# A float32 encoder block: the MLP's low parts all on VectorE, its unscaled stream kept in DRAM, the first gate products and the last stage's operands moved ahead

## The chip, the cores and the metric

The kernel runs on one core of a Trainium2 chip. The metric is the device time of one execution in microseconds (us). The kernel before took 1575.88 us (median of 3 runs, 1573.33 to 1576.59).

## What is computed

One encoder block on 1024 frames with 16 learned meta tokens in front, 1024 features wide, all in float32. A token mixer comes first and the change leaves it alone. What matters here is the gated MLP behind it and the final norm:

```
h = h + token_mixer(rmsnorm(h, g_mix))
u = rmsnorm(h, g_ffn)
a = causal_dwconv(u @ w_up, ffn_conv_w)          # 3 taps along time
h = h + (silu(a) * (u @ w_gate)) @ w_down        # 1024 -> 2816 -> 1024
out = rmsnorm(h, g_final)[:, 16:]                # rmsnorm(x,g) = x / sqrt(mean(x*x) + 1e-6) * g
```

## The kernel before

**Products in three parts.** TensorE (PE) multiplies in the reduced type fp32r. Every float32 operand is therefore split into a high part, a cast that ScalarE (ACT) makes, and a low part, the operand minus its high part. `mm3s` (L552) then issues three matmuls for each 128x128 weight block: high by high, high by low, low by high (L558 to L560). A split of weights is `wsplit` (L238, cast L242, subtraction L243); a split of activations is `rsplit` (L563, cast L565, subtraction L566). `wsplit` takes the engine of the subtraction as an argument. The mixer's output product and the whole down stage hand it VectorE (DVE). In the MLP `fstep` (L247) hands it VectorE for the first three units of weights and GpSimd (POOL) for all later ones.

**Seven products for eight.** Each large product is done by a scheme that needs seven block products instead of eight, from sums of weight blocks and sums of activation blocks. `fstep` makes the weight sums on VectorE (L261 to L263, L266), `xcomb` (L1035) the activation sums. The class `Seven` (L572) runs the products with w_out and w_down; `seven` (L1200) those with w_up and w_gate.

**The MLP.** The 2816 hidden features are 22 blocks of 128, taken as 11 pairs. Pair 0 is done with plain products while the activation sums are still being made (`first_up`, `first_gate`, L1300 to L1310); its results wait in DRAM and are finished by `first_out` (L1293) after pairs 1 to 4, one quarter after each. For pairs 1 to 10 `up_part` (L1312) makes seven products with w_up, each in two chunks of some 256 columns, and `gate_part` (L1323) seven with w_gate, each of 512 columns. The list PROD (L1199) says for each product which bank, weight unit and activation block it uses: the first two use blocks 0 and 1, which are plain, the third and fourth use sums that `xcomb` makes. ScalarE copies three of the intermediate banks to SBUF (tiles S0, S2 and S3, L1226), VectorE adds to them (L1230). The fifth product accumulates onto the bank that S2 was copied from, so it waits for that copy.

From a finished quarter of w_up `conv` (L1240) makes the depthwise convolution: one multiply (L1244) and two multiply-adds (L1246) on VectorE, Silu on ScalarE (L1247), and a multiply by Rb on GpSimd (L1248). `gate` (L1288) multiplies by the gate's quarter on VectorE and stores the result to DRAM.

**Why the multiply by Rb.** Rb holds 1/rms of each column. `scale_tasks` (L1075) scales the stream `resid` in place by Rb before the MLP, so the MLP's output has to be scaled too before it is added back to it (L1248). The final norm is then taken of a scaled stream: L1390 turns Rb into the epsilon that belongs to the scaled columns, `sq` (L1418) adds the squares onto it, and `final_rms` (L1426) calls `rms` with eps=False.

**The down stage.** It loops over five steps ("1", "2", "65", "73", "4") of 11 blocks each (L1391 to L1411 and L1445 to L1451). `prep` (L627) splits one step's operands ahead of its products `mms` (L674), one step early. After "73" `give` (L686) adds eight banks to `resid`. The last step "4" splits its w_down quarter when it comes to it, runs half of the columns inside the loop and the other half in `last_quarter` (L692) in two groups of 256.

**The end.** The final norm comes in three pieces of columns, 512, 256 and 256 (OP, L1416). For each, squares on ScalarE (L1423) are added on VectorE (piece 0) or GpSimd (pieces 1 and 2, L1424). `rms` (L297) sums over the partitions with matmuls (L304), takes the root (L310) and the reciprocal (L311), spreads the result over all partitions with matmuls into PSUM (L316), and copies it to Rb (L319). `final_out` (L1431) multiplies the blocks by gain and Rb: some in one instruction on VectorE (L1442), the others on ScalarE (gain, L1439) and GpSimd (Rb, L1440), and stores them.

**What sets the order.** Every engine, and the queue of SyncE (SP) that issues all DMAs, takes its instructions in order. The order is not that of the source: a scheduler built into the tile framework simulates the program and orders each engine's instructions by when they would be ready in that simulation. `after` (L81) adds an order between two instructions without a wait. Buffers come from rings of fixed length: split weights hi and lo 3 each (L131), raw weights 2, S tiles 5 (L1022), and two rings of four PSUM banks (L1055).

Of the kernel before, what the change touches and what calls it, by code (L numbers as in the profile page):

```python
# [17 lines left out]
P = 128  # L18
# [43 lines left out]
def body(ctx, tc, h_in, vecs, cst, mask_in, rot, w_v0, w_v, w_fm, w_out, w_up, w_gate, w_down, out):  # L62
# [172 lines left out]
    def fsplit(nm, srcs, eng=None):  # L235
        return wsplit(*split_tiles(nm), srcs, eng)

    def wsplit(hi, lo, srcs, eng=None):  # L238
        o = 0
        for x in srcs:  # L240
            n = x.shape[1]
            nc.scalar.copy(hi[:, o:o + n], x)  # L242
            (eng or nc.gpsimd).tensor_tensor(lo[:, o:o + n], x, hi[:, o:o + n].bitcast(F32), ALU.subtract)  # L243
            o += n
        return hi, lo

    def fstep(u, s):  # L247
# [6 lines left out]
        eng = V if u < 3 else None  # L254
        if u < 2:
            return fsplit(nm, [(r0, r1)[s]], eng)
        if s == 0:
            return fsplit(nm, [r0], eng)
        if s == 1:
# [37 lines left out]
    def rms(ss, t0, t1, nm, col, rb, ptags=("tr", "num"), eps=True):  # L297
# [5 lines left out]
        for i, (o, w) in enumerate(subs):  # L303
            nc.tensor.matmul(pc[:w, i:i + 1], ss[:, o:o + w], cs[:, C_M01 + P - 1:C_M01 + P], start=True, stop=True)  # L304
# [5 lines left out]
        nc.scalar.activation(col[:, i0:ns], pc[:, i0:ns], AF.Sqrt, bias=epsc if eps else 0.0, scale=1.0 / D)  # L310
# [8 lines left out]
        nc.scalar.copy(rb[:, x:], pr[:, :n - x])  # L319
# [243 lines left out]
    def rsplit(x, tiles):  # L563
        hi, lo = (t[:, :x.shape[1]] for t in tiles)
        nc.scalar.copy(hi, x)  # L565
        V.tensor_tensor(lo, x, hi.bitcast(F32), ALU.subtract)  # L566
        return hi, lo

# [3 lines left out]
    class Seven:  # L572
# [30 lines left out]
        def pre4(self, t):  # L603
# [3 lines left out]
            for i in range(2):  # L607
                self.four[t + i] = wsplit(*self.wfour(k + i), [x[:, i * HB:(i + 1) * HB]], V)
# [14 lines left out]
        def tsum(self, i, k):  # L623
            a, b, c = {1: ("A1", "B1", "A1"), 3: ("B1", "B1", "B2")}[i]
            V.tensor_tensor(self.act[a, k], self.act[b, k], self.act[c, k], ALU.subtract)

        def prep(self, t):  # L627
# [7 lines left out]
            if st == "4" and self.wfour:  # L635
# [4 lines left out]
            elif st == self.order[-1]:  # L640
                if k % 2 == 0:
                    self.w = d["w"]
                w = wsplit(*self.wlast(k), [self.w[:, k % 2 * HB:(k % 2 + 1) * HB]], V)
                self.ops[t] = [(w, self.rhalf(k, 0), "xy"[st == "2"])]
            elif st in self.QUARTER:
                if k % 2 == 0:
                    self.w = fsplit(nm, [d["w"]], V)
                r = rsplit(act[{"1": "A1", "2": "A2", "4": "A1"}[st], k], self.rt(st, k, 0))
                self.ops[t] = [(half_of(self.w, k % 2), r, "xy"[st == "2"])]
            elif st == "65":  # L650
# [3 lines left out]
                w = fsplit(nm, [d["l"]], V)  # L654
# [3 lines left out]
            else:  # L658
                w = fsplit(nm, [d["l"]], V)
# [5 lines left out]
        def rhalf(self, k, half):  # L665
            x = self.act["A2" if self.order[-1] == "2" else "A1", k][:, half * QT:(half + 1) * QT]
            return rsplit(x, self.rlast(k) if half else self.rt(self.order[-1], k, 0))
# [532 lines left out]
    def seven(kind, i, chunks, done):  # L1200

        S = {}
# [3 lines left out]
        for n, (bank, s, o, x) in enumerate(PROD):  # L1206
# [30 lines left out]
            elif n == 6:  # L1237
                done(1, 0, [banks["x", ci][:, :j1 - j0] for ci, (j0, j1) in enumerate(chunks)])

    def conv(i, m, half, c):  # L1240
        t0 = (TA, TB)[half]
# [6 lines left out]
        nc.gpsimd.tensor_tensor(cv, cv, Rb[:, t0 + 2:t0 + XW], ALU.mult)  # L1248
# [63 lines left out]
    def up_part(i):  # L1312
# [8 lines left out]
        seven("up", i, chunks, done)  # L1321

    def gate_part(i):  # L1323
        def done(m, half, c):
            gate(i, m, half, c[0] if isinstance(c, list) else c[:, :HALF])
        seven("ga", i, [(2, XW)], done)
        if i < 5:
            first_out((i - 1) % 2, (i - 1) // 2)
# [22 lines left out]
    def draw_(st, nm):  # L1351
        return raw_tile(nm) if st == "1" else dps["d"].tile([P, 2 * HB], F32, tag="draw", name="r" + nm, bufs=4)
# [7 lines left out]
    def dwlast(k):  # L1360
        if k < 6:
            if k % 2 == 0:
                dw4[k // 2] = split_tiles(f"d4_{k}")
            return half_of(dw4[k // 2], k % 2)
# [178 lines left out]
```

## Time and profile before

| | |
|---|---|
| median of 3 runs | 1575.88 us |
| time of the profiled execution | 1575.3 us |
| its span, first to last instruction | 1573.2 us |
| mean granted TensorE clock | 0.99 |
| PE / VectorE / ScalarE / GpSimd busy | 97 / 74 / 45 / 18% |
| HBM read and written | 142.25 and 45.13 MB, 119 GB/s |

Times in the trace count from the span's start. The mixer runs to about 740 us, its output product to about 875, the MLP's pair 0 to 920, its pairs 1 to 10 to about 1345, the down stage to 1561, and the end follows. A PE that the profile calls busy is not always at full speed: the granted clock has two levels, 2.4 GHz (shown as 1.00) and 1.2 GHz (0.50), and a stretch's mean lies between.

### The profile page before, as it was taken

How to read it: one execution, taken by the hardware profiler on the slowest of the kernel's cores; microseconds unless marked ns; L12 is line 12 of the kernel's file. 1: busy time of each engine (PE TensorE's matmuls, PEld its weight loads, DVE VectorE, ACT ScalarE, POOL GpSimd, SP SyncE). 2: the span in 40 equal slices, each digit the busy share in tenths (PEclk: the TensorE clock that was granted, in tenths of full speed). 3: DMA queues.
4: the chain of work that ended last, by engine and by line, in shares of the span. 5: the costliest groups of instructions: out<-in, count | busy, mean ns of one | idle time of the engine just before them, and what ended most of it. 6: DMA issues, size and time to landing. Idle time of an engine off the chain costs nothing.

```text
span 1573.2 us, 25559 instructions
## 1 busy us (share of the span) xinstructions
PE 1528.0 (97%) x9749; PEld 1398.2 (89%) x9749; DVE 1157.6 (74%) x2318; ACT 711.4 (45%) x1457; POOL 283.1 (18%) x195
## 2 busy tenths in 40 slices
PE   7999999999999999999999999999999999999996
PEld 6999999999999999997888988888999998888886
DVE  8767768597868686779976788877766666776575
ACT  6574655545242425355455453333333334333363
POOL 0000000000000000000000006666666665000006
PEclk9999999999999999999999999999999999999999
DMA  6125435262625353245430122222222224832312
GB/s 211 41 69 166 149 116 180 86 217 93 217 79 191 105 160 129 88 154 194 177 121 27 34 88 101 85 91 74 81 81 81 81 81 162 320 115 88 105 61 107
DMA packets 88315, 189.04 MB, mean 120 GB/s; under 512 B 8504, under 2 KB 29696, under 8 KB 88192
## 3 DMA queue, kind: packets, MB, share of 16 engines
q1 hardware_dynamic: 88192, 187.41, 35.3%
q8 instruction: 76, 1.25, 0.3%
q14 instruction: 47, 0.39, 0.1%
HBM read 142.25 MB, written 45.13 MB: 119 GB/s over the span
## 4 chain that ended last, share of the span: by engine, by line
PE 79%; DVE 8%; DMA 7%; ACT 3%; issue 2%; POOL 1%; SPq 0%; DVEq 0%; ACTq 0%; POOLq 0%
PE pv L380 3%; PE pv L381 3%; PE pv L382 3%; PE pga_x L558 2%; PE pup_x L559 2%; PE po L391 2%; PE po L392 2%; PE po L390 2%; PE pup_x L558 2%; PE pup_x L560 2%; PE pga_x L559 2%; PE pga_x L560 2%; PE pdx L559 2%; PE pdx L560 2%; PE pdx L558 2%
## 5 line engine op out<-in xcount | busy, mean ns | idle before, releaser
L1248 POOL TENSOR_TENSOR cv<-cv,Rb 128x512 f32<-128x512 f32 x44 | 67.6, 1541 | 980.3 <-ACT cv L1247 967.9
L380 PE MATMUL pv<-hi_v,uh 128*128 128x256 f32 (+1 forms) x512 | 146.5, 286 | 7.6 <-DVE uh L278 7.6
L382 PE MATMUL pv<-hi_v,ul 128*128 128x256 f32 (+1 forms) x512 | 144.9, 284 | 1.9 <-DVE ul L281 1.8
L381 PE MATMUL pv<-lo_v,uh 128*128 128x256 f32 (+1 forms) x512 | 145.4, 284 | 0.0
L390 PE MATMUL po<-uh,hi_o 128*128 128x386 f32 (+2 forms) x384 | 125.1, 326 | 0.0
L391 PE MATMUL po<-ul,hi_o 128*128 128x386 f32 (+2 forms) x384 | 123.2, 321 | 0.0
L392 PE MATMUL po<-uh,lo_o 128*128 128x386 f32 (+2 forms) x384 | 122.9, 320 | 0.0
L380 PEld LDWEIGHTS pv<-hi_v,uh 128*128 128x128 f32 x512 | 97.1, 190 | 10.3 <-ACT hi_v L149 7.2
L382 PEld LDWEIGHTS pv<-hi_v,ul 128*128 128x128 f32 x512 | 96.6, 189 | 2.4 <-DVE ul L281 2.3
L381 PEld LDWEIGHTS pv<-lo_v,uh 128*128 128x128 f32 x512 | 96.9, 189 | 1.0 <-DVE lo_v L150 0.9
L243 POOL TENSOR_TENSOR lo_ga<-fraw_ga,hi_ga 128x512 fp32r<-128x512 f32 (+1 forms) x50 | 87.8, 1765 | 43.9 <-ACT hi_ga L242 43.9
L243 POOL TENSOR_TENSOR lo_up<-raw_up,hi_up 128x512 fp32r<-128x512 f32 (+1 forms) x45 | 74.0, 1654 | 47.4 <-ACT hi_up L242 47.4
L242 ACT CAST hi_up<-raw_up 128x512 fp32r<-128x512 f32 (+1 forms) x52 | 36.5, 720 | 97.0 <-PE pga_z L559 45.7
L390 PEld LDWEIGHTS po<-uh,hi_o 128*128 128x128 f32 x384 | 72.5, 189 | 0.1
L391 PEld LDWEIGHTS po<-ul,hi_o 128*128 128x128 f32 x384 | 72.4, 188 | 0.2
L392 PEld LDWEIGHTS po<-uh,lo_o 128*128 128x128 f32 x384 | 72.2, 188 | 0.0
L559 PE MATMUL pup_x<-ul_g,hi_up 128*128 128x256 f32 (+1 forms) x240 | 68.2, 286 | 1.0 <-DVE ul_g L1011 1.0
L558 PE MATMUL pup_x<-uh_g,hi_up 128*128 128x256 f32 (+1 forms) x240 | 68.0, 285 | 0.6 <-ACT uh_g L1010 0.6
L560 PE MATMUL pup_x<-uh_g,lo_up 128*128 128x256 f32 (+1 forms) x240 | 66.7, 284 | 0.0
L390 PE MATMUL pq<-uh,hi_q 128*128 128x400 f32 (+2 forms) x192 | 63.9, 333 | 2.3 <-DVE vl L356 1.2
L242 ACT CAST hi_ga<-fraw_ga 128x512 fp32r<-128x512 f32 (+1 forms) x52 | 36.4, 718 | 62.4 <-PE pup_z L559 48.2
L390 PE MATMUL pk<-uh,hi_k 128*128 128x400 f32 (+2 forms) x192 | 62.4, 325 | 0.3 <-DVE rq L411 0.3
(733 smaller groups left out, 5198.9 us busy)
## 6 DMA issues: line engine op xcount, KB each, us to landing
wsd<-w_down_d SPq DMA_DIRECT2D x22, 512.0 KB, 4.2
wsd<-wsd SPq DMA_DIRECT2D x44, 256.0 KB, 2.3
raw_up<-w_up_d SPq DMA_DIRECT2D x22, 512.0 KB, 3.6
fraw_ga<-w_gate_d SPq DMA_DIRECT2D x22, 512.0 KB, 3.6
acts<-cv SPq DMA_DIRECT2D x44, 256.0 KB, 2.0
rd<-wsd SPq DMA_DIRECT2D x22, 512.0 KB, 3.2
wsw<-w_out_d SPq DMA_DIRECT2D x16, 512.0 KB, 4.2
raw_o<-w_fm_d SPq DMA_DIRECT2D x16, 512.0 KB, 3.5
```

The source lines that it names most:

```text
L242: nc.scalar.copy(hi[:, o:o + n], x)
L243: (eng or nc.gpsimd).tensor_tensor(lo[:, o:o + n], x, hi[:, o:o + n].bitcast(F32), ALU.subtract)
L380: nc.tensor.matmul(pv[:L, :nv], a, hi[:, o:o + nv], start=kb == 0, stop=False)
L381: nc.tensor.matmul(pv[:L, :nv], a, lo[:, o:o + nv], start=False, stop=False)
L382: nc.tensor.matmul(pv[:L, :nv], b, hi[:, o:o + nv], start=False, stop=kb == KB - 1)
L390: nc.tensor.matmul(pt[:, :n], a, uh[kb][:, t0:t1], start=kb == 0, stop=False)
L391: nc.tensor.matmul(pt[:, :n], a, ul[kb][:, t0:t1], start=False, stop=False)
L392: nc.tensor.matmul(pt[:, :n], b, uh[kb][:, t0:t1], start=False, stop=kb == KB - 1)
L558: m.append(nc.tensor.matmul(pt, ah, xh_, start=first and k == 0, stop=False, skip_group_check=True))
L559: nc.tensor.matmul(pt, ah, xl_, start=False, stop=False, skip_group_check=True)
L560: m.append(nc.tensor.matmul(pt, al, xh_, start=False, stop=last and k == n - 1, skip_group_check=True))
L1248: nc.gpsimd.tensor_tensor(cv, cv, Rb[:, t0 + 2:t0 + XW], ALU.mult)
```

## The change

- `wsplit` has no engine argument any more: VectorE makes every low part.
- `conv` makes its first multiply on ScalarE, and the multiply by Rb is gone. In its place `norm_tasks` (L1064) stores each block of the unscaled stream to DRAM, 24 DMAs in all, before it is scaled, and pairs 3 to 10 each end with one DMA of 512 KB that brings one block of it back to `resid`.
- In pair 1 the gate's first two products come behind the up product's first two; the unit of weights that they need, (3, 0), is split before (2, 1).
- In the down stage the last step's weights of blocks 6 to 10 are loaded and split during step "73", into memory that held activations; the first three blocks of the last step are prepared before `give`, the others three ahead instead of one. The second halves of the last step's activations are split in the loop, ordered behind the splits of the first halves, and the sums `tsum` are ordered behind the latest `rsplit`.
- In the end all adds of squares go to VectorE; in piece 2 the last block's squares are not added but summed by matmuls of their own. Pieces 0 and 1 are multiplied by the factor where it lies in PSUM, without the copy, all on VectorE. In piece 2 VectorE does the same for six blocks; for blocks 1 and 4 ScalarE applies the gain ahead of time and GpSimd the factor. Each piece is stored in four DMAs.

```diff
-    def wsplit(hi, lo, srcs, eng=None):
+    def wsplit(hi, lo, srcs):
...
-            (eng or nc.gpsimd).tensor_tensor(lo[:, o:o + n], x, hi[:, o:o + n].bitcast(F32), ALU.subtract)
+            nc.vector.tensor_tensor(lo[:, o:o + n], x, hi[:, o:o + n].bitcast(F32), ALU.subtract)
...
     fu = [(u, s) for u in range(len(fseq)) for s in range(2 if u < 2 else 4)]
+    fu.insert(fu.index((2, 1)), fu.pop(fu.index((3, 0))))
...
         for i, (o, w) in enumerate(subs):
-            nc.tensor.matmul(pc[:w, i:i + 1], ss[:, o:o + w], cs[:, C_M01 + P - 1:C_M01 + P], start=True, stop=True)
+            for a in (ss, *more):
+                nc.tensor.matmul(pc[:w, i:i + 1], a[:, o:o + w], cs[:, C_M01 + P - 1:C_M01 + P], start=a is ss, stop=a is (ss, *more)[-1])
...
-        nc.scalar.copy(rb[:, x:], pr[:, :n - x])
+        if rb is not None:
+            nc.scalar.copy(rb[:, x:], pr[:, :n - x])
+        return pr[:, :n - x]
...
             nc.scalar.activation(dst, resid[:, mb, t0:t1], AF.Square)
+            u0 = max(t0, META)
+            nc.sync.dma_start(stream[:, mb, u0 - META:t1 - META], resid[:, mb, u0:t1])
...
+            if n == 1:
+                yield
...
-        nc.vector.tensor_scalar(cv, c[:, 2:XW], vec[:, w + 2:w + 3], None, ALU.mult)
+        nc.scalar.activation(cv, c[:, 2:XW], AF.Copy, scale=vec[:, w + 2:w + 3])
...
         nc.scalar.activation(cv, cv, AF.Silu)
-        nc.gpsimd.tensor_tensor(cv, cv, Rb[:, t0 + 2:t0 + XW], ALU.mult)
...
     for i in range(1, NPAIR):
-        up_part(i)
+        u, g = up_part(i), gate_part(i)
+        next(u)
+        if i == 1:
+            next(g)
+        run(u)
...
-        gate_part(i)
+        run(g)
+        if 2 < i:
+            kb = i - 3
+            nc.sync.dma_start(resid[:, kb, META:], stream[:, kb])
...
-    nc.scalar.activation(Rb[:, META:], Rb[:, META:], AF.Square, scale=math.sqrt(EPS * D / P))
...
-            down.tsum(1, t - 2)
+            after(down.tsum(1, t - 2), last["rsplit"][1])
...
+        if st == "73":
+            for u, v in ((2, 6), (3, 8), (5, 10)):
+                if k == u:
+                    down.load(T4 + v)
+                if k == u + 2:
+                    down.pre4(T4 + v)
         down.mms(t)
         if k == KD - 1:
+            if st == "73":
+                for u in range(T4, T4 + 3):
+                    down.prep(u)
             down.give(st)
...
-        (G if p else V).tensor_tensor(ss, ss, dst, ALU.add)
+        if p == 2 and mb == KB - 1:
+            lastsq.append(dst)
+        else:
+            V.tensor_tensor(ss, ss, dst, ALU.add)
...
+        for mb in pool:
+            nc.gpsimd.tensor_tensor(resid[:, mb, a0:t1], resid[:, mb, a0:t1], R[1], ALU.mult)
...
-                if mb in pool:
-                    nc.scalar.activation(x, x, AF.Copy, scale=g)
-                    nc.gpsimd.tensor_tensor(x, x, R, ALU.mult)
-                else:
-                    nc.vector.scalar_tensor_tensor(x, x, g, R, ALU.mult, ALU.mult)
+                if mb not in pool:
+                    V.scalar_tensor_tensor(x, x, vec[:, V_FIN + mb:V_FIN + mb + 1], R[0], ALU.mult, ALU.mult)
...
-    down.prep(T4)
     for k in range(KD):
         down.load(T4 + k + 4)
-        down.prep(T4 + k + 1)
+        down.prep(T4 + k + 3)
+        down.late[k] = down.rhalf(k, 1)
         down.mms(T4 + k)
...
-            final_rms(0)
-            final_out(0, (1, 3, 5, 7), (0, 4, 8))
-        final_rms(p)
-        final_out(p, (1, 3, 5, 7) if p == 1 else (2, 5, 7), (0, 4, 8) if p == 1 else (0, 3, 6, 8))
+            final_out(0, final_rms(0), (), (0, 2, 4, 6, 8))
+        else:
+            for mb in (1, 4):
+                x = resid[:, mb, OP[2][0]:OP[2][1]]
+                nc.scalar.activation(x, x, AF.Copy, scale=vec[:, V_FIN + mb:V_FIN + mb + 1])
+        final_out(p, final_rms(p), (1, 4) if p == 2 else (), (0, 2, 4, 6, 8))
```

## Rows read from the trace of the kernel before

**Rows 1.** Two long stretches of the MLP: length, engines' busy time, granted clock.

```profile
942.00:1110.00 168.00, 159.38 (x970) 141.94 (x969) 133.83 (x147) 58.12 (x109) 107.46 (x67) 0.97 0.27 90
1110.00:1330.00 220.00, 219.95 (x1393) 197.91 (x1391) 152.93 (x182) 80.03 (x151) 146.63 (x90) 1.00 0.25 84
```

**Rows 2.** What PE waited for, 820 to 1345 us: total us, times, longest.

```profile
PE pga_x L558 <- ACT s2ga L1226: 9.4, 5, 2.7
```

**Rows 3.** Timeline of ScalarE, 947 to 963 us; idle time in brackets.

```profile
959.38 1.29 ACT L1247 ACTIVATE cv<-cv 128x512 f32<-128x512 f32 x2 [6.02 <-DVE cv L1246]
960.58 0.57 ACT L1226 COPY s2ga<-pga_x 128x512 f32<-128x512 f32 x1
```

**Rows 4.** VectorE's groups, 942 to 1330 us: count, busy us, mean ns.

```profile
L261 DVE TENSOR_TENSOR s<-raw_up 128x512 f32<-128x512 f32 x9 | 16.0, 1781 | 0.0
...
L1246 DVE SCALAR_TENSOR_TENSOR cv<-s3up,vec,cv 128x512 f32<-128x512 f32 x20 | 14.9, 745 | 0.0
...
L1244 DVE TENSOR_SCALAR cv<-s0up,vec 128x512 f32<-128x512 f32 x9 | 4.4, 487 | 0.3
```

**Rows 5.** VectorE's low parts while GpSimd rests, 1345 to 1520 us.

```profile
L243 DVE TENSOR_TENSOR lo_d<-rd,hi_d 128x1024 fp32r<-128x1024 f32 x27 | 33.0, 1221 | 29.2 <-ACT hi_d L242 29.2
...
L243 DVE TENSOR_TENSOR lo_d<-rd,hi_d 128x512 fp32r<-128x512 f32 x3 | 2.0, 690 | 3.7 <-ACT hi_d L242 3.7
```

**Rows 6.** GpSimd's groups, 942 to 1330 us: first and last of six of L243.

```profile
L243 POOL TENSOR_TENSOR lo_ga<-fraw_ga,hi_ga 128x512 fp32r<-128x512 f32 x40 | 63.8, 1608 | 25.8 <-ACT hi_ga L242 25.8
...
L243 POOL TENSOR_TENSOR lo_ga<-s,hi_ga 128x512 fp32r<-128x512 f32 x10 | 14.8, 1475 | 0.0
```

**Rows 7.** Timeline of VectorE, 947 to 962 us: start, us, what.

```profile
951.01 1.79 DVE L261 TENSOR_TENSOR s<-raw_up 128x512 f32<-128x512 f32 x1
...
959.27 0.74 DVE L1246 SCALAR_TENSOR_TENSOR cv<-c0b,vec,cv 128x512 f32<-128x512 f32 x1
```

**Rows 8.** Short stretches around PE's pauses, columns as in rows 1.

```profile
930.00:942.00 12.00, 9.49 (x44) 8.06 (x43) 7.37 (x16) 6.18 (x13) 2.80 (x2) 0.72 0.15 44
958.00:966.00 8.00, 5.27 (x18) 3.97 (x17) 6.79 (x8) 3.17 (x5) 5.30 (x3) 0.79 0.39 131
1002.00:1010.00 8.00, 6.05 (x24) 4.64 (x23) 6.78 (x8) 3.17 (x5) 5.30 (x3) 0.79 0.37 132
1044.00:1048.00 4.00, 2.01 (x10) 1.32 (x8) 3.96 (x7) 1.82 (x4) 1.14 (x1) 1.00 0.04 5
1086.00:1096.00 10.00, 8.05 (x33) 6.28 (x32) 8.79 (x10) 3.17 (x5) 5.28 (x3) 0.83 0.28 101
...
1524.00:1530.00 6.00, 4.13 (x32) 3.66 (x31) 6.00 (x13) 3.69 (x8) 0.00 (x0) 1.00 0.00 1
1552.00:1554.00 2.00, 0.63 (x6) 0.42 (x5) 2.00 (x4) 0.17 (x1) 2.00 (x2) 1.00 0.96 369
```

**Rows 9.** ScalarE's groups, 1530 us to the end.

```profile
L1439 ACT ACTIVATE resid<-resid,vec 128x512 f32<-128x512 f32 x3 | 2.2, 717 | 0.0
...
L319 ACT COPY Rb<-prc 128x256 f32<-128x256 f32 x2 | 0.7, 364 | 1.1 <-PE prc L316 1.1
```

**Rows 10.** A stretch of the down stage, columns as in rows 1.

```profile
1345.00:1520.00 175.00, 175.00 (x756) 141.82 (x755) 120.25 (x169) 74.33 (x113) 0.00 (x0) 1.00 0.39 138
```

**Rows 11.** DMA issues: count, KB each, median us to landing.

```profile
acts<-cv SPq DMA_DIRECT2D x44, 256.0 KB, 2.0
```

**Rows 12.** Timeline of PE, 1560.6 us to the end.

```profile
1563.03 0.61 PE L304 MATMUL pcc<-cs,Rb 128*128 128x1 f32 x4 [1.90 <-POOL Rb L1424]
```

**Rows 13.** VectorE's groups, 1530 us to the end.

```profile
L1442 DVE SCALAR_TENSOR_TENSOR resid<-resid,vec,Rb 128x256 f32<-128x256 f32 x9 | 7.1, 846 | 2.6 <-ACT Rb L319 2.6
...
L705 DVE TENSOR_TENSOR resid<-pdx,resid 128x256 f32<-128x256 f32 x8 | 3.1, 418 | 4.4 <-PE pdx L560 4.4
```

**Rows 14.** Timeline of SP's DMA queue, 850 to 880 us.

```profile
860.51 9.55 SPq L231 DMA_DIRECT2D fraw_ga<-w_gate_d  x3
```

**Rows 15.** Timeline of VectorE, 855 to 862 us.

```profile
856.27 4.93 DVE L1082 TENSOR_TENSOR resid<-resid,Rb 128x514 f32<-128x514 f32 x8 [4.89 <-ACT Rb L319]
```

More of the change, by code (lines that the diff above doesn't have):

```diff
@@ L233, in fetch, with fsplit @@
         fraws[u] = r
[L235 to L238 removed]
+    def fsplit(nm, srcs):
+        return wsplit(*split_tiles(nm), srcs)
+    def wsplit(hi, lo, srcs):
         o = 0
@@ L295, in sumsq, with rms @@
         return spare_tile("ss", "ss" + nm)
-    def rms(ss, t0, t1, nm, col, rb, ptags=("tr", "num"), eps=True):
+    def rms(ss, t0, t1, nm, col, rb, ptags=("tr", "num"), more=()):
         n = t1 - t0
@@ L561, in mm3s, with rsplit, behind @@
         return m[0], m[-1]
-    def rsplit(x, tiles):
+    def rsplit(x, tiles, late=False):
         hi, lo = (t[:, :x.shape[1]] for t in tiles)
-        nc.scalar.copy(hi, x)
-        V.tensor_tensor(lo, x, hi.bitcast(F32), ALU.subtract)
+        m = nc.scalar.copy(hi, x), V.tensor_tensor(lo, x, hi.bitcast(F32), ALU.subtract)
+        if late:
+            behind(m)
+        else:
+            last["rsplit"] = m
         return hi, lo
+    def behind(m):
+        for x, y in zip(m, last["rsplit"]):
+            after(x, y)
     def half_of(u, o):
@@ L606, in pre4 @@
             x = self.draws[t]["w"]
-            for i in range(2):
-                self.four[t + i] = wsplit(*self.wfour(k + i), [x[:, i * HB:(i + 1) * HB]], V)
+            for i in range(x.shape[1] // HB):
+                self.four[t + i] = wsplit(*self.wfour(k + i), [x[:, i * HB:(i + 1) * HB]])
             self.read(t, True)
@@ L634, in prep @@
             act = self.act
-            if st == "4" and self.wfour:
+            if st == "4" and self.order[-1] != "4":
                 if t not in self.four:
@@ L641, in prep @@
                 if k % 2 == 0:
-                    self.w = d["w"]
-                w = wsplit(*self.wlast(k), [self.w[:, k % 2 * HB:(k % 2 + 1) * HB]], V)
+                    self.w = d.get("w")
+                w = self.four.get(t) or wsplit(*self.wlast(k), [self.w[:, k % 2 * HB:(k % 2 + 1) * HB]])
                 self.ops[t] = [(w, self.rhalf(k, 0), "xy"[st == "2"])]
@@ L666, in rhalf @@
             x = self.act["A2" if self.order[-1] == "2" else "A1", k][:, half * QT:(half + 1) * QT]
-            return rsplit(x, self.rlast(k) if half else self.rt(self.order[-1], k, 0))
+            return rsplit(x, self.rlast(k) if half else self.rt(self.order[-1], k, 0), half and self.nm == "d")
         def bank(self, b, j, new=False):
@@ L1060, in fps @@
         return pp(nm, ring[-1])
+    stream = dram.tile([P, KB, SEQ], F32, name="stream")
     def norm_tasks(t0, t1, mbs=range(KB), first=True):
@@ L1087, in run @@
         for f in fs:
-            f()
+            if f:
+                f()
     for p in range(3):
@@ L1320, in done @@
             conv(i, m, half, c)
-        seven("up", i, chunks, done)
+        return seven("up", i, chunks, done)
     def gate_part(i):
@@ L1325, in done @@
             gate(i, m, half, c[0] if isinstance(c, list) else c[:, :HALF])
-        seven("ga", i, [(2, XW)], done)
-        if i < 5:
-            first_out((i - 1) % 2, (i - 1) // 2)
+        return seven("ga", i, [(2, XW)], done)
     dps = {}
@@ L1360, in dwlast, with dfour @@
     def dwlast(k):
[L1361 to L1364, printed above, removed]
-        return tuple(dps["e"].tile([P, HB], F32R, tag=f"w4{x}{k}", name=f"w4{x}{k}") for x in "hl")
+        if k % 2 == 0:
+            dw4[k // 2] = split_tiles(f"d4_{k}")
+        return half_of(dw4[k // 2], k % 2)
+    def dfour(k):
+        r = []
+        for i in (2 * k - 12, 2 * k - 11):
+            tag = ("ul1", "uh2", "ul2")[i // 4]
+            if tag not in dw4:
+                dw4[tag] = upool.tile([P, 2 * T], F32R, tag=tag, name=f"{tag}_w4")
+            r.append(dw4[tag][:, i % 4 * HB:(i % 4 + 1) * HB])
+        return tuple(r)
     down = Seven("d", KD, w_down, ("1", "2", "65", "73", "4"), META, draw_, drt,
@@ L1403, in body @@
         if 2 <= t < KD + 2:
-            down.tsum(1, t - 2)
+            after(down.tsum(1, t - 2), last["rsplit"][1])
         if KD + 4 <= t < 2 * KD + 4:
-            down.tsum(3, t - KD - 4)
+            after(down.tsum(3, t - KD - 4), last["rsplit"][1])
         if st != "1" or k + 4 < KD:
             down.load(t + 4)
+        if st == "73":
[4 more added lines that the diff above has]
+                    down.pre4(T4 + v)
         down.mms(t)
         if k == KD - 1:
+            if st == "73":
+                for u in range(T4, T4 + 3):
+                    down.prep(u)
             down.give(st)
```

44 lines of the change are left out of this document (24 added, 20 removed).

## The prediction, made before the changed kernel had run

> **What bounds the kernel now.** I read the busy shares, then the busy time by stretch, then the pauses of PE, the waits behind them and what the late engines did. PE is busy nearly throughout, so VectorE, ScalarE and GpSimd matter only where they make PE pause. In pairs 5 to 10 PE has no pause: 219.95 of 220 us; in the stretch of pairs 1 to 4 it lacks 8.6 of 168 us and its clock is 0.97 [rows 1]. The reader is to see that a pause costs twice: PE stands still, and the clock is then granted at its lower level (1.2 of 2.4 GHz) for some us. A stretch of length L at mean clock c does L(1-c) less work.
>
> Who is late? Most of the waiting in the MLP is one product waiting for ScalarE's copy S2 [rows 2]. At 958 us ScalarE sat idle 6.02 us until VectorE had finished two convolutions, ran two Silus, and only then copied S2 [rows 3], though the bank had been complete for some time. VectorE was late because it ran beside GpSimd: a plain two-input instruction on 128x512 takes 1781 ns there [rows 4], with GpSimd at rest 690 [rows 5]. A multiply-add of the convolution takes 745 where it is undisturbed [rows 4]. Pairs 1 to 4 carry one quarter of pair 0 more each than pairs 5 to 10, and VectorE is busy 80% there (133.83 of 168) against 70% (152.93 of 220) [rows 1].
>
> **The change, part by part.** All sums are against the profiled execution: 1575.3 us, that is 1573.2 of span and 2.1 around it; the median of the runs is 0.6 higher.
>
> *Low parts and multiplies, pairs 1 to 10.* VectorE gains 95 subtractions of 512 columns and 19 of 1024 (six groups of L243 [rows 6]): 95 x 0.690 + 19 x 1.221 [rows 5] = 88.7 us. It loses 43 multiplies (L1244, 487 ns where undisturbed [rows 4]), and GpSimd's 254.1 us [rows 1] disappear, with the slowing of VectorE. The 286 VectorE instructions that stay (329 less 43 [rows 1]) cost, undisturbed, 86 x 0.745 (conv) + 143 x 0.690 (512 columns) + 57 x 0.42 (256) = 186.7 us. So VectorE goes from 286.8 to about 275 of 388 us, 71%; in pairs 1 to 4 to about 73%, near the 70% at which pairs 5 to 10 run without a pause now. The slowing is worth 286.8 - 186.7 - 43 x 0.487 = 79 us; if half of it stayed, VectorE would be busy 81%: that is what the slower rival is made of.
>
> The chain to S2 at 958 us, redone: from 951 to the end of the last conv instruction VectorE took 9.0 us [rows 7]. Undisturbed and without the two multiplies that is 2 x 0.69 + 4 x 0.745 = 4.4 us. The low parts add 88.7 / 388 of the time, 2.1 us in 9. So it ends 2.5 us earlier in the same order, while PE's pause was 2.73 [rows 8]. But the order is made anew by a simulation that plainly did not count on the slowing, and now nothing is left that slows VectorE. I take these pauses as gone but for one of 2 us.
>
> Their price [rows 8]: idle 2.73 + 1.95 + 1.99 + 1.95 = 8.6; clock 8 x 0.21 + 8 x 0.21 + 0 + 10 x 0.17 = 5.1. Together 13.7, of which I count 11.7. The bounds are a gain of 13.7 and a loss, in the slower rival.
>
> *ScalarE's multiplies.* 43 at 0.717 [rows 9] are 30.8 us more on an engine busy 138.2 of 388 us [rows 1]; 44% after. Hidden by its idle time; without that cover it delays S2, the same rival. Here a rule speaks against the change. An undisturbed multiply costs VectorE 487 ns [rows 4] and ScalarE 717 [rows 9], 0.23 us more each, 9.9 us in all, off PE's path. The Trainium skill ("ScalarE: Activation LUTs", Rules for kernel authors) tells authors to do a plain multiply on VectorE and not on ScalarE; by it this part would be a loss of those 9.9 us of engine time. The trace bears out the prices, not that they reach PE.
>
> *Gate products first in pair 1.* From 930 to 942 us PE lacks 2.51 us and runs at 0.72, 12 x 0.28 = 3.4: 5.9 us [rows 8], waiting for `xcomb`. Two gate products are 24 matmuls of 512 columns at 0.23 us (756, nearly all of that size, in 175 us of the down stage [rows 10]), 5.5 us of work that needs no sums, against 2.5 us of waiting. They need unit (3, 0) split earlier, 1.22 us on VectorE, but the three splits and sums of unit (2, 1) then come after it. I count all 5.9; the bounds are 0 and 5.9.
>
> *Stream through DRAM.* 24 stores and 8 loads on a queue that carries 84 to 90 GB/s in the MLP [rows 1]. VectorE's scaling of a block now waits for the block's store: 2.0 us from issue to landing for 256 KB [rows 11]. Between the last store and the first scaling lie the norm's sum, root, spreading matmuls and copy, on three engines, so I take 0; the upper bound is in the rival on the queue. No gain can come of it. The reloads are needed only by the down stage. Nothing waits on them.
>
> *Last step.* From 1524 to 1530 us PE lacks 1.87 us [rows 8], waiting for low parts while VectorE also ran `give`. With three blocks prepared before it I count 1.9 (bounds 0 and 1.9). Six weight splits move forward, none is added; in "73" PE is never short.
>
> *The end.* The pause of 1.37 us at 1552 [rows 8] waits for a reciprocal behind four multiplies of piece 0 on VectorE. They become eight, but undisturbed: I count half, 0.7 (bounds 0 and 1.4). Behind the last product, at 1561.1, PE waits 1.90 us for the add of squares on GpSimd [rows 12]. The bank's add takes 0.42 of it [rows 13] and the square about as much; of the rest 0.8 goes with the add. Two more matmuls on the path take back 0.3 (0.61 for four [rows 12]). The copy of the factor, 0.36 [rows 9], leaves VectorE's path. Five last multiplies of 846 ns, 4.2 us, become six. How fast? In this same stretch an instruction with one operand in PSUM took 418 ns while those with both in SBUF took 846 [rows 13]: six then take 2.5, and the end gains 0.5 + 0.4 + 1.7 = 2.6. The Trainium skill ("SBUF — State Buffer", Who interferes with whom) says that VectorE contends with GpSimd only with two SBUF inputs or in its two-port modes; by that the 2.5 holds and GpSimd's two blocks cost nothing. If they were slowed all the same, six take 5.1 and the end gains nothing. I keep 0 to 2.6 as bounds.
>
> Sum: 11.7 + 5.9 + 1.9 + 0.7 + 2.6 = 22.8. 1575.3 - 22.8 = 1552.5. About 0.2%, 3 us, is what a measurement of this kernel can tell from no change.
>
> **Rivals.** (a) The scheduler makes its own order, so the moved gate products may not be issued early, or the weights for them are late. For it: PE already issues matmuls out of source order. Against it: they become ready early. Then 5.9 stays: 1558.4 us.
>
> (b) The S2 pauses stay, because VectorE, with the low parts, ends its convolutions only 2.5 us earlier (above). For it: that arithmetic. Against it: pairs 5 to 10 at 70%. Then 11.7 is lost: 1564.2.
>
> (c) The SP queue. A group of weight fetches is issued there at 860.5 us, when its buffers come free; VectorE scales the stream's second half from 856.3 on, for PE's first products [rows 14, 15]. If the stores of that half stand behind those fetches in the queue, scaling starts when they have landed, at about 862.5 to 864.5, 8 us late at most, and PE pauses as long, with 3.4 us of clock as at 930: 1552.5 + 11.4 = 1563.9. For it: the queue takes its DMAs in order. Against it: the stores are ready some time before 856.
>
> (d) Slower. In every pair ScalarE's queue holds a conv multiply and a Silu, both waiting for a VectorE that now also has the low parts, ahead of S2. If all ten pairs pause as two of pairs 1 to 4 do now, 1.95 and 1.7 of clock, that is 36.5 us instead of 13.7: 1575.3 + 22.8 - 11.1 (the other terms) = 1587. It decides at (13.7 + 11.1) / 3.65, from seven pausing pairs on. For it: one such wait of 6.02 us [rows 3]. Against it: 71% load and nothing that slows VectorE.
>
> **How the numbers follow.** Chances: forecast 0.65 (1546 to 1556: all gains taken whole give 1549.8, and the new order elsewhere may shift 3 us), (a) 0.12, (b) 0.10, (c) 0.05, (d) 0.08. The range to 1565 takes in (a), (b) and (c) and leaves (d) out. Faster: all but (d) and a little, 0.91; same 0.02; slower 0.07.
>
> **What would show it.** GpSimd at rest until the end, with VectorE's L243, L261 and conv instructions at 0.69 and 0.75 in the MLP, and VectorE near 71%. PE without a wait for S2 and at clock 1.00 from the MLP's start to the end of the down stage. Gate products before the third up product in pair 1. No pause at the start of the last step. From PE's last product to the end 9.5 us instead of 12.1 (1573.2 less 1561.1). The prediction is wrong if PE waits for S2 in many pairs, if scaling waits for a DMA, or if VectorE's instructions stay slow with GpSimd idle.

## The result, and the profile after

The changed kernel takes 1551.45 us (median of 4 runs, 1548.61 to 1553.86), the kernel before 1576.24 (1573.33 to 1577.94): a ratio of 0.9844, 95% interval 0.9821 to 0.9866. The profiled execution took 1551.88 us, span 1550.1.

GpSimd is at rest up to the end, and VectorE has kept its share of the span. The first part of the page (busy us, share, instructions):

```profile
PE 1519.3 (98%) x9753; PEld 1395.5 (90%) x9753; DVE 1125.6 (73%) x2409; ACT 733.8 (47%) x1489; POOL 2.4 (0%) x12
```

The gain lies in the MLP. The stretch from PE's first up product of pair 1 to its first down product holds 2511 matmuls in both kernels. Before, columns as in [rows 1] (length; busy time of PE, of its weight loads, of VectorE, ScalarE and GpSimd; granted clock):

```profile
919.90:1336.40 416.50, 404.61 (x2511) 362.57 (x2510) 307.95 (x374) 155.27 (x295) 257.24 (x158) 0.98 0.27 90
```

and after:

```profile
925.20:1319.90 394.70, 394.10 (x2511) 356.85 (x2510) 273.67 (x444) 182.66 (x339) 0.00 (x0) 1.00 0.33 106
```

That is 21.8 us less: 11.3 of idle time (11.9 before, 0.6 after) and 10.5 because the same matmuls run at clock 1.00 throughout. What PE still waits for from 820 us to the end (total, times, longest), against [rows 2]:

```profile
PE pcc L305 <- ACT sqc L1463: 0.8, 1, 0.8
PE prc L317 <- DVE rcolc L312: 0.6, 1, 0.6
PE pup_x L561 <- ACT uh_g L1021: 0.4, 1, 0.4
```

S2 is gone from the list. The view of one tile shows it best: who waited for the ten copies S2 of the gate, before (weight loads of PE, PEld, stand apart from its matmuls),

```profile
who waited for it (us, times):
  PEld pga_x L558: 13.0, 10
  PE pga_x L558: 9.4, 5
```

where the same view of the changed kernel names nobody. So before, in all ten pairs, the weight load of the next product into that bank waited for the copy, and pairs 5 to 10, which look free of pauses in [rows 1], ran at the edge of one. The fifth of PE's five waits, 0.8 us, falls in pair 10, just behind the second stretch of [rows 1].

VectorE's instructions of the MLP, 942 to 1305 us, are undisturbed (count, busy us, mean ns; [rows 4, 5] before):

```profile
L243 DVE TENSOR_TENSOR lo_ga<-fraw_ga,hi_ga 128x512 fp32r<-128x512 f32 x39 | 26.5, 683 | 0.1
...
L1263 DVE SCALAR_TENSOR_TENSOR cv<-s2up,vec,cv 128x512 f32<-128x512 f32 x20 | 15.0, 749 | 3.0 <-ACT cv L1261 3.0
...
L243 DVE TENSOR_TENSOR lo_ga<-fraw_ga,hi_ga 128x1024 fp32r<-128x1024 f32 x9 | 11.0, 1226 | 35.2 <-ACT hi_ga L242 35.2
```

ScalarE's timeline in pair 1, where [rows 3] had 6.02 us of idle time and two Silus ahead of S2:

```profile
954.06 0.71 ACT L1261 ACTIVATE cv<-c0b,vec 128x512 f32<-128x512 f32 x1
954.70 0.63 ACT L1264 ACTIVATE cv<-cv 128x512 f32<-128x512 f32 x1
955.27 0.59 ACT L1242 COPY s2ga<-pga_x 128x512 f32<-128x512 f32 x1
956.69 0.63 ACT L1264 ACTIVATE cv<-cv 128x512 f32<-128x512 f32 x1 [0.84 <-DVE cv L1263]
```

Two things differ: nothing is late, and in pair 1 S2 now stands ahead of two of the Silus (the scheduler's new order). Pairs 2 to 4 have the old order, S2 behind both Silus; in pair 2 ScalarE now waits for PE ahead of S2:

```profile
992.36 1.15 ACT L1264 ACTIVATE cv<-cv 128x512 f32<-128x512 f32 x2
994.87 0.59 ACT L1242 COPY s2ga<-pga_x 128x512 f32<-128x512 f32 x1 [1.35 <-PE pga_x L563]
```

Why nothing is late, the experiments have to say.

The last step, from the last product of "73" to the last of all, takes 33.8 us instead of 38.2. The tail, timeline of all engines, against [rows 12, 13]; sqc are squares, pcc their sums over the partitions, rcolc the reciprocal, prc the factor spread in PSUM:

```profile
1540.82 0.42 ACT L1463 ACTIVATE sqc<-resid 128x256 f32<-128x256 f32 x1 [3.92 <-DVE resid L716]
...
1541.28 0.38 PE L305 MATMUL pcc<-cs,sqc 128*128 128x1 f32 x2 [0.82 <-ACT sqc L1463]
...
1543.65 0.37 ACT L321 COPY Rb<-prc 128x256 f32<-128x256 f32 x1 [1.23 <-PE prc L317]
1544.05 2.44 DVE L1485 SCALAR_TENSOR_TENSOR resid<-resid,vec,prc 128x256 f32<-128x256 f32 x6 [1.44 <-ACT Rb L321]
1544.10 1.41 POOL L1480 TENSOR_TENSOR resid<-resid,Rb 128x256 f32<-128x256 f32 x2 [1542.54 <-ACT Rb L321]
```

PE's last product ends at 1540.3, so the end takes 9.8 us instead of 12.1. From the first up product of pair 1 to the end it is 624.9 us (1550.1 less 925.2) instead of 653.3: 28.4 us less, more than the 24.8 between the medians and the 23.1 between the two spans. The rest went ahead of pair 1, which this profile reached 5.3 us later: the mixer, which the change leaves alone, was 7.1 us longer in it.

### The profile page after: what moved, and what is told of

Same layout as the page of the kernel before. It is cut to its first block, busy times and chain, and to the rows that moved or that the text cites. A ratio compares the mean times of both kernels' runs of the same rounds, so it can differ in the third digit from the quotient of the medians.

```text
span 1550.1 us, 25437 instructions
## 1 busy us (share of the span) xinstructions
PE 1519.3 (98%) x9753; PEld 1395.5 (90%) x9753; DVE 1125.6 (73%) x2409; ACT 733.8 (47%) x1489; POOL 2.4 (0%) x12
## 4 chain that ended last, share of the span: by engine, by line
PE 85%; DMA 7%; DVE 5%; ACT 2%; issue 1%; SPq 0%; DVEq 0%; ACTq 0%
PE pv L383 4%; PE pv L384 3%; PE pv L385 3%; PE pdx L561 3%; PE pdx L563 3%; PE pdx L562 3%; PE pup_x L562 2%; PE pup_x L563 2%; PE pga_x L561 2%; PE pga_x L563 2%; PE pga_x L562 2%; PE pup_x L561 2%; PE po L394 2%; PE po L395 2%; PE po L393 2%; PE pdy L561 2%
## 5 line engine op out<-in xcount | busy, mean ns | idle before, releaser
L243 DVE TENSOR_TENSOR lo_ga<-fraw_ga,hi_ga 128x512 fp32r<-128x512 f32 (+1 forms) x52 | 41.9, 808 | 37.7 <-ACT hi_ga L242 37.6
L243 DVE TENSOR_TENSOR lo_up<-raw_up,hi_up 128x512 fp32r<-128x512 f32 (+1 forms) x52 | 41.4, 809 | 36.5 <-ACT hi_up L242 35.7
L394 PE MATMUL pq<-ul,hi_q 128*128 128x400 f32 (+2 forms) x192 | 62.7, 326 | 0.0
L395 PE MATMUL pq<-uh,lo_q 128*128 128x400 f32 (+2 forms) x192 | 62.4, 325 | 0.0
```

Source lines behind the costliest of these rows:

```text
L243: nc.vector.tensor_tensor(lo[:, o:o + n], x, hi[:, o:o + n].bitcast(F32), ALU.subtract)
L394: nc.tensor.matmul(pt[:, :n], a, ul[kb][:, t0:t1], start=False, stop=False)
L395: nc.tensor.matmul(pt[:, :n], b, uh[kb][:, t0:t1], start=False, stop=kb == KB - 1)
```

## The experiments

**The mixer: the same kernel again.**

> The changed kernel once more, for its mixer. PE's instructions up to the first product of pair 1 stand in the same order in both kernels, yet that stage ended 7.1 us later in the changed kernel's profile (first product of the output weights at 707.7 instead of 700.6 us), where ScalarE waited 4.26 us for a weight of the mixer instead of 2.63. Theory: that is how a DMA happened to land in one execution, so this profile may show 700 to 708 us there and a total between 1544 and 1554 us. Rival: the change itself delays it (longer program, other addresses), so it is 707 to 708 again, with the same wait of about 4.3 us. Both expect the MLP to run as before: pair 1's first product to the first down product 394 to 396 us, no wait of PE for S2.

1547.08 us (ratio 0.9825, 0.9802 to 0.9848). The first output product comes at 700.8 us. What ScalarE waited for, 345 to 365 us, in the first profile of the changed kernel,

```profile
ACT hi_v L149 <- DMA raw_v<-w_v_d: 5.8, 2, 4.3
```

and in this one:

```profile
ACT hi_v L149 <- DMA raw_v<-w_v_d: 4.2, 2, 2.6
```

One 512 KB weight landed 7.1 us after its issue in the one and 5.2 in the other (5.3 in the kernel before). How that transfer happened to land is the larger part of the difference: from 345 to 400 us PE is busy 52.36 us at clock 0.94 in the first profile and 54.45 at 1.00 in the second, some 5 us. The clock of the first 100 us, 0.97 against 1.00, is some 3 us more, and 400 to 550 us gives 1.5 back. Nor does every long mixer come from this wait: in the profile of gate_order_old it is 2.4 us and the first output product comes at 706.0. Over the profiles with this order of the mixer the first output product comes between 700.6 and 707.7 us. Stretches say more than totals here.

**Each part taken out of the changed kernel.**

```
 def fstep(u, s):
+    eng = nc.gpsimd if u > 2 else None
...
-    return fsplit(nm, [r0])
+    return fsplit(nm, [r0], eng)
```

> The changed kernel with the low parts of pairs 1 to 10 back on GpSimd; the multiplies by the norm's factor stay away and ScalarE keeps the convolution's multiplies. Theory (GpSimd beside VectorE makes VectorE late, and through ScalarE's queue the copy S2): the 114 low parts keep GpSimd busy some 170 us in the MLP, VectorE's 512-column instructions are again at 1.2 to 1.8 us where they fall beside it, PE waits for S2 again in pairs 1 to 4 and the clock falls: 5 to 13 us slower than the changed kernel, 1556 to 1565. Rival (the pauses went because the multiplies went off VectorE and GpSimd, or because the order was made anew): no wait for S2, within 2 us of the changed kernel.

```
     nc.scalar.activation(cv, cv, AF.Silu)
+    nc.gpsimd.tensor_tensor(cv, cv, Rb[:, t0 + 2:t0 + XW], ALU.mult)
```

> The changed kernel with a multiply by the norm's factor on GpSimd behind each Silu put back (43 or so of 512 columns); the factor is then in the result twice, which costs no time of its own. Theory: some 70 us of GpSimd work slow VectorE by 20 to 25 us, so VectorE stands near 75% in the MLP, below the 80% at which the kernel before paused: 0 to 4 us slower than the changed kernel. If it is 8 or more slower with waits for S2, the multiplies alone were the cause and the low parts' move was not needed; if the subtractions stay at 0.69 us beside it, the slowing is not GpSimd's doing.

```
-    nc.scalar.activation(cv, c[:, 2:XW], AF.Copy, scale=vec[:, w + 2:w + 3])
+    nc.vector.tensor_scalar(cv, c[:, 2:XW], vec[:, w + 2:w + 3], None, ALU.mult)
```

> The changed kernel with the convolution's first multiply back on VectorE (43 by 0.49 us, where ScalarE takes 0.72). By the rule that a plain multiply belongs on VectorE (the Trainium skill, ScalarE: Activation LUTs, Rules for kernel authors) 30.8 us leave ScalarE and 21 go to VectorE. Theory: VectorE goes from 69% to about 75% of the MLP, ScalarE from 45% to 37%, and PE still has no pause: within 2 us of the changed kernel, so where the multiply stands did not matter. Rival: VectorE's queue is the tight one, and at 75% one or more waits for S2 come back: 3 to 8 us slower.

| kernel | us (ratio, interval) | pair 1 to down stage | waits for S2 |
|---|---|---|---|
| changed | 1551.45 and 1547.08 | 394.7, 394.6 | none |
| low_on_gpsimd | 1551.30 (0.9847, 0.9828 to 0.9866) | 396.4 | none |
| mult_on_gpsimd | 1551.28 (0.9844, 0.9829 to 0.9859) | 395.0 | none |
| conv_mult_on_vector | 1547.17 (0.9811, 0.9796 to 0.9826) | 394.9 | none |

None of the three brings the waits for S2 back, against what I expected of low_on_gpsimd. There VectorE is about as slow as before where it meets GpSimd (group of VectorE, 942 to 1305 us):

```profile
L261 DVE TENSOR_TENSOR s<-raw_up 128x512 f32<-128x512 f32 x9 | 15.0, 1663 | 0.0
```

It is not free, though: the stretch is 1.8 us longer, and PE's weight loads now wait for another copy, S0 (915 to 1325 us), which they do in neither profile of the changed kernel:

```profile
PEld pga_x L562 <- ACT s0ga L1243: 2.8, 8, 0.4
```

And in mult_on_gpsimd VectorE is busy 130.69 of 163 us, the 80% at which the kernel before paused:

```profile
942.00:1105.00 163.00, 162.56 (x1063) 148.65 (x1064) 130.69 (x189) 77.27 (x142) 31.79 (x21) 1.00 0.32 105
```

So neither the slowing nor VectorE's share brings the pauses by itself. In conv_mult_on_vector VectorE's time between 942 and 1105 us rose from the 118.31 us of the changed kernel's second profile to 126.13, and ScalarE's fell from 77.34 to 63.04; PE is indifferent.

**Each part put alone into the kernel before, and an order alone.** The first three take one part of the change each.

```
-        eng = V if u < 3 else None
+        eng = V
```

> The kernel before with one part of the change: all low parts on VectorE; GpSimd keeps the multiplies by the norm's factor (some 70 us), the convolution stays on VectorE. VectorE by the rows: 186.7 + 88.7 + 21 us and some 22 of slowing, 318 of 388 us, 82%, no less than the 80% of the kernel before. Theory 1 (pauses for S2 come with VectorE's load): they stay, 1572 to 1580. Theory 2 (they come from what stands ahead of S2 in the two queues, and how slow that is; in this kernel's ScalarE order S2 stands ahead of the two last Silus in pair 1 where it stood behind them): most of the 13.7 us goes, 1562 to 1567.

```
-    nc.gpsimd.tensor_tensor(cv, cv, Rb[:, t0 + 2:t0 + XW], ALU.mult)
```

> The kernel before with the multiply by the norm's factor behind each Silu left out (the MLP's product then lacks that factor); low parts stay on GpSimd, whose work falls from 254 to some 180 us, and ScalarE's order is as before, S2 behind both Silus. Theory 1 (load): VectorE falls from 74% to about 68% of the MLP, so the pauses of pairs 1 to 4 go: 1562 to 1566. Theory 2 (queue ahead of S2): the same VectorE instructions stand ahead of S2 and the low parts still slow them, so half of the pauses or more stay: 1567 to 1575.

```
-    nc.vector.tensor_scalar(cv, c[:, 2:XW], vec[:, w + 2:w + 3], None, ALU.mult)
+    nc.scalar.activation(cv, c[:, 2:XW], AF.Copy, scale=vec[:, w + 2:w + 3])
```

> The kernel before with the convolution's first multiply on ScalarE alone; GpSimd keeps its 254 us. Two of the instructions that stood ahead of the pair's last Silus on VectorE (1.51 us each beside GpSimd at 952.73 us) leave it. Theory 1 (load): VectorE falls from 74% to some 67%, the pauses go, 1562 to 1566. Theory 2 (queue ahead of S2): 3.0 us less ahead of the Silus against a pause of 2.73 in pair 1 and 1.95 after it, so they go too: 1562 to 1566. Rival (the slowing by GpSimd is what matters, however long the queue): they stay within half: 1568 to 1576.

The fourth moves no work; `last["s3ga"]` is the gate's add to S3 of the pair:

```
 def conv(i, m, half, c):
-    nc.vector.tensor_scalar(cv, c[:, 2:XW], ...)
+    f = nc.vector.tensor_scalar(cv, c[:, 2:XW], ...)
+    if i == 0:
+        after(f, last["s3ga"])
```

> The kernel before with an order alone changed: the convolution of pair 0's quarter in pairs 1 to 4 starts on VectorE behind the gate's add to S3, so that it no longer stands ahead of S2. No work moves, GpSimd keeps its 254 us and slows VectorE as before. Theory 1 (load, slowing): VectorE is as busy as before, so pauses of the same size stay or move: 1571 to 1578. Theory 2 (what stands ahead of S2): four multiplies and multiply-adds of some 5.7 us leave the queue ahead of S2 and the S2 pauses go, with the 13.7 us or most of it: 1561 to 1566.

| kernel | us (ratio, interval) | pair 1 to down stage | PE's waits for S2 |
|---|---|---|---|
| before | 1575.87 | 416.5 | 9.4 us, 5 times |
| before_low_on_vector | 1559.66 (0.9897, 0.9873 to 0.9921) | 399.2 | none |
| before_no_mult | 1563.40 (0.9919, 0.9888 to 0.9950) | 401.3 | none (but 2.1 us once for S0) |
| before_conv_on_scalar | 1563.67 (0.9918, 0.9897 to 0.9939) | 404.4 | 1.4 us, once |
| before_pair0_later | 1564.73 (0.9925, 0.9901 to 0.9950) | 403.3 | 1.3 us, twice |

Any single part takes 12 to 17 of the 21.8 us. The last row is the telling one. There GpSimd is as busy and VectorE as slow as before (945 to 1110 us, and VectorE's group, 945 to 1330 us; 1781 ns in [rows 4]):

```profile
945.00:1110.00 165.00, 164.48 (x1053) 148.59 (x1052) 129.39 (x157) 61.70 (x117) 116.53 (x71) 1.00 0.28 93
```

```profile
L261 DVE TENSOR_TENSOR s<-raw_up 128x512 f32<-128x512 f32 x9 | 16.1, 1784 | 0.0
```

yet PE lacks 0.52 of 165 us. The view of the tile S2 shows how near the edge it still runs:

```profile
who waited for it (us, times):
  PEld pga_x L558: 4.4, 10
  PE pga_x L558: 1.3, 2
```

So the load theory fails: it expected 1571 to 1578 there, and 1572 to 1580 for before_low_on_vector, where VectorE is busy 133.74 us between 945 and 1110, 81%, without a wait for S2. But theory 2 as I had written it fails too, in before_no_mult: it expected half of the pauses or more to stay, 1567 to 1575, and 1563.40 came, within the load theory's range. ScalarE's order there is the old one in all ten pairs. In pair 1, against [rows 3]:

```profile
957.46 1.29 ACT L1247 ACTIVATE cv<-cv 128x512 f32<-128x512 f32 x2 [2.79 <-DVE cv L1246]
958.66 0.57 ACT L1226 COPY s2ga<-pga_x 128x512 f32<-128x512 f32 x1
```

VectorE's part of the chain, from its first multiply for these two Silus to the end of its last multiply-add, takes 5.2 us there (952.94 to 958.10) and took 7.3 (952.73 to 960.01), because GpSimd rests beside most of it. So both things count: what stands ahead of S2 in the two queues, the convolution of pair 0's quarter last of all, and how long each instruction takes beside GpSimd. Together they were 2 to 3 us too long, and whatever takes about that much away ends all or most of the pauses, be it instructions, their order or the slowing. (Pair 0's convolution is three instructions, 3.0 us in pair 1; the four of 5.7 us in the expectation were miscounted.) One wait of the same kind is left in before_no_mult, for S0 in pair 1:

```profile
PE pga_x L558 <- ACT s0ga L1226: 2.1, 1, 2.1
```

**Pair 1's order.**

```
-    fu.insert(fu.index((2, 1)), fu.pop(fu.index((3, 0))))
...
-        if i == 1:
-            next(g)
```

> The changed kernel with pair 1's products in the old order: the gate's first two products behind all of the up products, its first weight unit split where it was. Theory: PE's waits for VectorE's sums of pair 1 come back, 2.0 to 2.8 us of idle between 920 and 945 us with the clock at 0.86 to 0.93 there, as in all four kernels made from the one before: 4 to 6 us more from the first output product to the first down product than the 612 to 614 us of the changed kernel. Rival (VectorE without GpSimd beside it makes the sums early enough): no idle there, 0 to 1 us.

1554.31 us (0.9849, 0.9829 to 0.9870). Pair 1 to the down stage is 398.5 us, 3.9 more; from the first output product, by which the expectation counts, it is 618.1 against 612.2 and 614.5. The window, and what PE waited for (uh_g and ul_g are the high and low parts of the activation sums):

```profile
920.00:945.00 25.00, 22.84 (x167) 21.44 (x166) 20.32 (x48) 16.84 (x38) 0.00 (x0) 0.93 0.69 231
```

```profile
PE pup_z L561 <- DVE ul_g L1024: 1.2, 1, 1.2
PE pup_x L560 <- ACT uh_g L1020: 0.9, 2, 0.5
```

2.16 us of idle, where the changed kernel has 0.60, and 0.07 of 25 us of clock, 1.75: this gain is the order's, and a VectorE without GpSimd beside it does not replace it.

**The last step.** `dwlast` and the tiles are as in the kernel before, and:

```
-        if st == "73":
-            for u, v in ((2, 6), (3, 8), (5, 10)):
...
-                for u in range(T4, T4 + 3):
-                    down.prep(u)
...
-        down.prep(T4 + k + 3)
-        down.late[k] = down.rhalf(k, 1)
+        down.prep(T4 + k + 1)
```

What stays is `rsplit`'s `late`, by which the second halves' splits stand behind the others, and the order of `tsum`.

> The changed kernel with the last step's operands split as in the kernel before: nothing of it ahead of the additions of give, the second halves split in the last quarters. From the last product of step 73 to the last product of all it took 38.2 us before and 33.8 after. Theory: the wait of 1.9 us for VectorE's low parts at the step's start comes back and nothing else, since the pause of 1.4 us at 1552 us hung on the multiplies of piece 0, which stay as changed: 35.5 to 36 us. Rival (the second halves split ahead are what freed VectorE there): 37 to 38.2 us.

1550.70 us (0.9830, 0.9809 to 0.9852). The step takes 34.5 us, 0.7 more than 33.8, less than either expectation: the pause of 1.9 us does not come back (0.2 us). Columns as in [rows 8], where the kernel before had 4.13 of 6.00 us:

```profile
1500.00:1508.00 8.00, 7.79 (x67) 7.59 (x66) 7.97 (x17) 6.42 (x15) 0.00 (x0) 1.00 0.01 2
```

The likely reason is where VectorE made the low parts of the second halves (tile r4l). In the kernel before, whose last step begins at 1522.9 us:

```profile
L566 DVE TENSOR_TENSOR r4l<-uh_d,r4h x7: 411/417/419, 1515.4 to 1521.3; 128x256 fp32r<-128x256 f32 x7
L566 DVE TENSOR_TENSOR r4l<-ul_d,r4h x4: 412/416/418, 1517.0 to 1519.1; 128x256 fp32r<-128x256 f32 x4
```

In last_step_old, whose last step begins at 1499.7:

```profile
L568 DVE TENSOR_TENSOR r4l<-uh_d,r4h x7: 421/423/427, 1511.7 to 1515.0; 128x256 fp32r<-128x256 f32 x7
L568 DVE TENSOR_TENSOR r4l<-ul_d,r4h x4: 422/422/425, 1513.0 to 1514.0; 128x256 fp32r<-128x256 f32 x4
```

Before, eleven low parts of second halves, some 4.2 us of work that PE needs only from 1541.7 on, stood ahead of first halves that it waited for at 1526. In last_step_old all of them come after the step's start. No run undid the `late` order alone, so this reading rests on the two traces.

**The end.**

```
-  V.scalar_tensor_tensor(x, x, vec[...], R[0], ALU.mult, ALU.mult)
+  V.scalar_tensor_tensor(x, x, vec[...], R[1] if pool else R[0], ALU.mult, ALU.mult)
```

> The changed kernel with the last piece's six multiplies on VectorE reading the norm's factor from its copy in SBUF, where they read it from PSUM (six in 2.44 us, 0.41 each, beside GpSimd's two). Theory (two operands in SBUF are what is slowed beside GpSimd): the first multiplies, beside GpSimd, take 0.7 to 0.85 us each and the six 3.3 to 4.5 us, so the end from the last product is 10.8 to 12 us instead of 9.9. Rival (they were fast because GpSimd has only two blocks): 2.5 to 2.7 us for the six, no change.

1548.65 us (0.9819, 0.9803 to 0.9835). Timeline of the last multiplies:

```profile
1542.06 3.49 DVE L1485 SCALAR_TENSOR_TENSOR resid<-resid,vec,Rb 128x256 f32<-128x256 f32 x6 [1.27 <-ACT Rb L321]
1542.11 1.58 POOL L1480 TENSOR_TENSOR resid<-resid,Rb 128x256 f32<-128x256 f32 x2 [1540.56 <-ACT Rb L321]
```

Six in 3.49 us instead of 2.44, and GpSimd's two in 1.58 instead of 1.41: 1.05 us for VectorE, 0.8 for the end (10.7 us from the start of the last product, 9.9 in the changed kernel's second profile). The operand's place is what counts; the six are at the low side of what was expected, the end just below it. In the time of the whole kernel it does not show.

**A try at more.**

```
-        nc.sync.dma_start(a, src[k])
-        nc.sync.dma_start(b, src[k + n])
+        for x in (nc.sync.dma_start(a, src[k]), nc.sync.dma_start(b, src[k + n])):
+            after(x, last["vload"])
```

and every third sum made after the next head's V product; `last["vload"]` is the latest load of a weight for V.

> A try at a faster version. The changed kernel whose profiles end the mixer at 700.6 to 707.7 us, by how late one 512 KB weight for V lands near 355 us (5.2 to 7.1 us after its issue, behind two loads for the sums of the down weights in SP's queue). Here the loads for these sums are held behind the weights for V of the head, and one sum of three is made a stage later. If that wait is the cause, ScalarE's wait of 2.6 to 4.3 us for the weight shrinks below 1 us, the first output product comes at 697 to 701 us and the whole at 1542 to 1548 us with less spread. Rival: the sums made later delay something else in the mixer, and it is 1547 to 1556.

1549.10 us (0.9822, 0.9803 to 0.9842), no faster than the changed kernel; the first output product comes at 704.3 us. ScalarE's waits for the weight are still there:

```profile
ACT hi_v L151 <- DMA raw_v<-w_v_d: 4.3, 2, 2.9
```

PE had no idle time there (50.00 of 50 us from 350 to 400), but was idle 1.99 us between 200 and 300, where it was idle 0.31 in the changed kernel's second profile. The rival held. No run here is clearly faster than the changed kernel.

## Why the prediction was right, and where its working was not

1552.5 was predicted, 1551.45 came. The agreement is partly luck: the terms were 5.6 us too small (22.8 against 28.4 by the trace from pair 1 on), and the mixer was 7.1 us longer in the first profile. The same kernel again took 1547.08, near the lower end of the 1546 to 1556 that I gave.

*The pauses for S2* (13.7 priced, 11.7 counted): the whole MLP gave 21.8; without pair 1's order, 3.9, that is 17.9. The price was low by three terms of some 2 us each: the clock was summed from short stretches, 5.1 + 3.4 us [rows 8], where the whole stretch shows 10.5; the pause of 2 us held back did not stay; and some 2 us priced under pair 1's order went with the other parts. The step that failed is the yardstick. The chain was read rightly: ScalarE sat idle 6.02 us behind VectorE, ahead of two Silus and S2 [rows 3], a copy that needed neither; and that VectorE was late because it ran beside GpSimd is borne out by before_no_mult. But I took VectorE's busy share as the measure of what would pause, 73% against 80. mult_on_gpsimd runs at 80% and before_low_on_vector at 81% without a wait for S2, and before_pair0_later keeps GpSimd's work and the slowing and loses most of the pauses. What counts is how long the chain ahead of S2 is. An order alone gave 13.2 of the 21.8 us, and each move of work, taken back by itself, cost at most 1.8 in that stretch.

*The convolution's multiplies on ScalarE* (counted as hidden): hidden, as conv_mult_on_vector shows. The rule of the Trainium skill ("ScalarE: Activation LUTs", Rules for kernel authors) that a plain multiply belongs on VectorE makes no difference in time there, 394.9 against 394.6 us. In the kernel before the move that goes against it gained 12.1 us (before_conv_on_scalar, 416.5 to 404.4), where it took multiplies of VectorE out of the chain ahead of S2.

*The gate's products first* (5.9, bounds 0 and 5.9): 3.9. The place and mechanism were right; about 2 us of pair 1's loss went with the other parts. before_low_on_vector, which keeps the old order, has 0.93 there for the 0.86 of the kernel before.

*The stream through DRAM* (0): nothing on the list of PE's waits comes from it, and VectorE's scaling waits for the factor (12.6 us in all, 12.2 before) and not for a DMA.

*The last step* (1.9 for its start, 0.7 for the pause at 1552): 4.4, of which 3.24 is idle time (1.87 and 1.37) and the rest that the same products keep PE busy 33.80 us instead of 34.96. The size was too small and the cause largely wrong: splitting ahead gave 0.7; the rest of the first term goes, as far as the two traces show, to the order of the second halves' splits. I had not costed that part of the diff. The second pause went whole, 1.4, though the reciprocal stands behind eight multiplies now. Two things did it, and no run parts them. The eight took 5.35 us where four had taken 6.05, so the reciprocal comes 4.5 us after the start of that piece's sums (1528.62 to 1533.14) instead of 6.3 (1547.34 to 1553.66). And the matmuls that need it come 7.2 us after those sums (1528.6 to 1535.8) where PE was ready for them after 5.2. By these numbers, as an estimate, either alone would have been enough.

*The end* (2.6): 2.3. The multiplies were mis-sized: five of them took 3.57 us, not 4.2 (846 ns is a mean over nine [rows 13]), so six in 2.44 give 1.1, not 1.7. PE's wait for the squares fell from 1.90 us to 0.82, by 1.1 where 0.8 was taken. The copy of the factor did not leave VectorE's path: its first multiply starts at 1544.05, 0.03 us after the copy from the same bank ends. The Trainium skill ("PSUM — Partial Sum Buffer", PSUM bank collisions raise a hardware error) says that two engines must not access one bank at the same time and that the compiler's scheduler orders such accesses, reads too; these rows agree. The Trainium skill ("SBUF — State Buffer", Who interferes with whom) says that a VectorE instruction with at most one SBUF input, outside the two-port modes, does not contend with GpSimd; 2.44 us against 3.49 bears that out.

## What to carry to other kernels

Before an engine's busy share is made the measure, look at what stands ahead of the late instruction in its queue, and in the queue of whoever it waits for, and at how long each of these takes; a copy that frees a bank should not stand behind work that nobody needs yet. Look at the weight loads' waits too: they show a stage that runs at the edge of a pause while its matmuls show none (ten pairs against five here). And when several parts of a change each remove the same wait, taking them out one at a time finds that none is needed; put them in one at a time as well.

## What was not expected of the hardware

The same instructions of the mixer took up to 7.1 us more or less (700.6 to 707.7 us), about as much as some edits are worth: in the profile where one 512 KB weight landed 1.9 us later, PE's pause behind it grew from 0.6 to 2.6 us and its clock between 350 and 375 us stood at 0.86. And VectorE's slowing beside GpSimd, 1663 ns for a two-input instruction that takes 690 alone, cost only 1.8 us of 396 in low_on_gpsimd, and no wait for S2.
